# Moving x and the result in one transfer per quarter, and the norm's sums ahead of x times norm_g on GpSimd

## The chip, the core and the metric

The kernel runs on 1 core of one Trainium2 chip. The metric is the device time of one execution in microseconds. The engines go by the names of the profile: PE is TensorE's matmul side and PEld its weight loads, DVE is VectorE, ACT is ScalarE, POOL is GpSimd, and SP issues most of the DMA transfers. An engine's own queue of DMA issues is written SPq, ACTq or POOLq.

## The reference

Four pre-norm residual layers over x of 256 rows and 1024 columns, and one norm at the end. The layers' mixers are pooling, gated DeltaNet, latent attention and pooling again.

```python
def rmsnorm(x, g):
    xf = x.astype(jnp.float32)
    y = xf * lax.rsqrt(jnp.mean(xf * xf, axis=-1, keepdims=True) + EPS)
    return (y * g.astype(jnp.float32)).astype(x.dtype)

for i in range(DEPTH):
    h = rmsnorm(x, norm_g[i])
    y = mixer(i % 3)(h, ...)
    x = x + y.astype(x.dtype)
return rmsnorm(x, final_g)
```

The change touches how x comes in, how the result goes out, and the norm between a layer and the next.

## The kernel before

**Tiles.** x lives in two tiles of 128 partitions, `xs[0]` and `xs[1]` (named x_93 and x_94 in the listings of instructions below), 1024 columns and one more. Partitions 0 to 63 hold the even rows of a block of 128, partitions 64 to 127 the odd ones. Half a tile, 512 columns, is called a quarter of x here, written x(t,c) for tile t and column half c. Every number that is multiplied on TensorE is split into a high and a low part: ACT makes `whi` (or `hTh`) by a cast, DVE the difference `wlo` (or `hTl`), and three matmuls replace one.

**Order of the work.** The program is written for all engines in one order, with `later(...)` putting a piece of it behind a given instruction. A scheduler then sorts each engine's instructions by a simulated time. So an edit in one place may also change the order elsewhere. Each engine works its own list strictly in order.

**Start.** `load_x` (line 304) issues two transfers per quarter on SP's queue, each of 64 rows. Between the quarters stand the first weight units (`prefetch`, line 1348): the first projection, the gate of pooling group 3, takes its 8 row blocks of weights as units 0 to 3 of one block each (256 KB) and units 4 and 5 of two (512 KB). `First.feed` (line 355) transposes a quarter on TensorE (line 359) and splits it (lines 242 and 247). The square sums of the four quarters (line 256) run on ACT between weight splits (line 153).

**End of a layer.** `layer_out` (line 445) makes the output projection in two column halves. For the second half the result comes in two pieces of 256 columns per tile. As soon as a piece is complete, DVE adds it to x (line 450), and `part_done` (line 285) adds its squares: ACT squares and sums (line 256), POOL works on the sum of one number per partition. With the first piece of a tile's second half POOL also computes `half`: a multiplication by D (line 297) and a root (line 298), stored in the extra column of x, so that the last square sum, over 257 columns, comes out complete. `Normed.begin` (line 382) multiplies x by norm_g on POOL for 256 columns, called `hg`, and `Normed.rest` (line 388) takes the inverse root `xr` on POOL (line 390) and multiplies by it: two pieces on ACT (line 402) and two on DVE (line 397).

**The result.** `Final.feed` (line 437) is the same norm with final_g. For each of the two tiles it issues four transfers on SP's queue (line 442): two column halves of 64 even and 64 odd rows.

Of the kernel before, what the change touches and what calls it, by code (L numbers as in the profile page):

```python
# [13 lines left out]
ALU = mybir.AluOpType  # L14
# [3 lines left out]
D = 1024  # L18
S = 256
NT = S // P  # L20
KD = D // P
CW = 512
CUT = 256
KU = 2
EPS = 1e-6
# [17 lines left out]
def trunk(ctx: ExitStack, tc: tile.TileContext, x, positions, norm_g, pool_w_in, pool_w_grp,  # L43
          pool_scale, pool_w_out, gdn_w_in, gdn_conv, gdn_a_log, gdn_dt_bias, gdn_norm_g,
          gdn_w_out, mla_w_in, mla_q_norm_g, mla_w_uq, mla_kv_norm_g, mla_w_ukv, mla_w_out,
          final_g, out, depth=4, final=True):
    nc = tc.nc
# [28 lines left out]
    def small(name, *dims, bufs=2):  # L76
        return sm.tile([P, *dims], F32, tag=name, name=name, bufs=bufs)
# [4 lines left out]
    def later(*instructions):  # L82

        order = ExitStack()
        for ins in instructions:
            order.enter_context(tc.issue_after(ins))
        return order


    mark = {}  # L90
# [74 lines left out]
    def unpaired(o, ps, n=CW):  # L165

        return halves(o, n), parted(ps, n)
# [86 lines left out]
    def sumsq(src, n, o, scale=1.0):  # L254
        junk = wh.tile([P, CW + 1], F32, tag="junk", name="junk", bufs=1)
        nc.scalar.activation(junk[:, :n], src, AF.Square, scale=scale, accum_out=o)
# [25 lines left out]
    xs = [const.tile([P, D + 1], F32, name=f"x{t}") for t in range(NT)]  # L282
    ms = [None] * NT

    def part_done(t, a, n, apart=False):
        s = small(f"ms{t}{a // 256}", 1)
        end = a + n == D
        more = int(end and not apart)
        with later(*[m for e, m in mark.items() if e == "rest"]):
            sumsq(xs[t][:, a:a + n + more], n + more, s, scale=float(D) ** -0.5)  # L290
        if a == 0:
            nc.gpsimd.tensor_scalar(s, s, EPS, None, ALU.add)
        elif not more:
            nc.gpsimd.tensor_tensor(out=s, in0=s, in1=ms[t], op=ALU.add)
        ms[t] = s
        if a and not end:
            nc.gpsimd.tensor_scalar(s, s, float(D), None, ALU.mult)
            nc.gpsimd.tensor_tensor(out=xs[t][:, D:], in0=s, in1=half, op=ALU.pow)

    def by_row(a, t):  # L300

        return a[0, t * P:(t + 1) * P, :].rearrange("(a b) c -> b a c", b=2)

    def load_x(t, c):
        sl = slice(c * CW, (c + 1) * CW)
        for b in range(2):
            nc.sync.dma_start(out=xs[t][b * 64:(b + 1) * 64, sl], in_=by_row(x, t)[b, :, sl])

    load_x(0, 0)
    grow = small("grow", P, bufs=1)[:KD]  # L310
    nc.scalar.dma_start(out=grow, in_=norm_g[0].rearrange("(k p) -> k p", p=P))
# [4 lines left out]
    half = const.tile([P, 1], F32, name="half")  # L316
# [23 lines left out]
    class First:  # L340
# [14 lines left out]
        def feed(self, t, c):  # L355
            ps = bank(tps, "tp")
            for b in range(4):
                a = c * CW + b * P
                nc.tensor.transpose(ps[:, b * P:(b + 1) * P], xs[t][:, a:a + P], ident)
            return split_out((ps.rearrange("p (b s) -> p b s", b=4),  # L360
                              self.hT.many(4 * c, 4, t * P, P), None))
# [63 lines left out]
    def cols_of(w, c0, cols=CW):  # L425
        v = w.rearrange("(k p) c -> p k c", p=P)
        return lambda k0, n: v[:, k0:k0 + n, c0:c0 + cols]
# [5 lines left out]
    class Final(Normed):  # L433
# [3 lines left out]
        def feed(self, t):  # L437
            y = self.rest(t) if final else [xs[t][:, :CW], xs[t][:, CW:D]]
            for c in range(2):
                sl = slice(c * CW, (c + 1) * CW)  # L440
                for b in range(2):
                    nc.sync.dma_start(out=by_row(out, t)[b, :, sl],
                                      in_=y[c][b * 64:(b + 1) * 64])

    def layer_out(w, yT, ks, i, gain=None):

        def done(t, a, ps):
            n = ps.shape[1]
            xv, pv = unpaired(xs[t][:, a:a + n], ps, n)
            nc.vector.tensor_tensor(out=xv, in0=pv, in1=xv, op=ALU.add)  # L450
            part_done(t, a, n)

        project(cols_of(w, 0), ks, yT, done=lambda t, c, ps: done(t, 0, ps), gain=gain)
        with later(mark["sp"]):
            nxt = LayerIn(i + 1) if i + 1 < depth else Final()
        for t in range(NT):
            nxt.begin(t, 0)

        def last(t, c, ps):
            done(t, CW + c * CUT, ps)  # L460
            if c == 0:
                nxt.begin(t, CW)
            else:
                nxt.feed(t)

        project(cols_of(w, CW), ks, yT, tail=3, cuts=CW // CUT, done=last, gain=gain)
        return nxt
# [885 lines left out]
    nxt = First()  # L1353
    nxt.columns()
    turn = nxt.feed(0, 0)
    with later(*turn):
        prefetch(0)
        warming(WARM[1])
        prefetch(1)
    load_x(1, 0)  # L1360
    with later(mark["act"], mark["dve"]):
        turn = nxt.feed(1, 0)
    with later(*turn):
        prefetch(2)
        prefetch(3)
        part_done(0, 0, CW, apart=True)
    load_x(0, 1)
    load_x(1, 1)
    with later(mark["act"], mark["dve"]):
        turn = nxt.feed(0, 1)  # L1370
        turn += nxt.feed(1, 1)
    with later(*turn):
        prefetch(4)
        part_done(1, 0, CW, apart=True)
        part_done(0, CW, CW, apart=True)
        prefetch(5)
        part_done(1, CW, CW, apart=True)
    for i in range(depth):
        nxt = layers[i % 3](i, i // 3, nxt.hT)
# [31 lines left out]
```

## Time and profile before

| | us |
|---|---|
| median of 3 runs (lowest to highest) | 828.32 (827.48 to 829.5) |
| the profiled execution's own time | 832.1 |
| its span, first to last instruction | 830.4 |
| PE busy | 799.4 (96%) |
| DVE busy | 603.4 (73%) |
| ACT busy | 492.9 (59%) |
| POOL busy | 159.8 (19%) |
| DMA, mean over the span | 168 GB/s |

A line of a timeline gives the start, the length, the engine, the line of the kernel, the operation, output and input tiles, their shape, a count, and in brackets how long the engine had been idle and for what. A line of a tile or line view gives the shortest, median and longest duration in ns, and when the first and the last started. A DMA issue is given with the size and the median time from issue to landing. PE's matmuls overlap, so its busy share says less than which wait ends last. The granted clock of the profiled execution was 0.986 of full speed.

### The profile page before, as it was taken

The numbers are of one execution on the slowest core, as the hardware profiler recorded it, in microseconds if no ns is written. First come the engines' busy times: TensorE is split into PE (matmuls) and PEld (weight loads), VectorE is DVE, ScalarE is ACT, GpSimd is POOL, SyncE is SP. The second block draws the span as 40 slices with busy tenths as digits, with TensorE's granted clock in tenths as the row PEclk, the third lists the DMA queues.
The fourth block names the chain that finished last, engine by engine and source line by source line (L and its number), as shares of the span: only waits on it lengthen the run. The fifth ranks groups of instructions, "written<-read, shape, count | busy, mean of one in ns | idle before, by whom it ended". The sixth has DMA issues, their size and how long they took to land.

```text
span 830.4 us, 16162 instructions
## 1 busy us (share of the span) xinstructions
PE 799.4 (96%) x5966; PEld 758.0 (91%) x5966; DVE 603.4 (73%) x1141; ACT 492.9 (59%) x993; POOL 159.8 (19%) x296
## 2 busy tenths in 40 slices
PE   8989999999898979999999999999999999999996
PEld 7989988989898978788989999999999989999996
DVE  4699887666987967356666678778877767877772
ACT  6665565567855655255566564666665565566662
POOL 2001100334236992023121112000000120000012
PEclk9999999999999989899999999999999999999998
DMA  6865666756655544303647786653552547576662
GB/s 204 224 180 167 193 209 210 221 153 195 193 135 180 163 139 118 124 12 115 187 125 224 231 180 185 192 164 102 153 175 80 179 143 214 183 223 202 202 204 51
DMA packets 109079, 139.90 MB, mean 168 GB/s; under 512 B 21316, under 2 KB 51208, under 8 KB 109000
## 3 DMA queue, kind: packets, MB, share of 16 engines
q1 hardware_dynamic: 106608, 137.12, 55.0%
q0 software_dynamic: 528, 1.58, 0.6%
q8 instruction: 47, 0.77, 0.4%
q10 hardware_dynamic: 1864, 0.17, 0.2%
q14 instruction: 32, 0.26, 0.1%
HBM read 137.27 MB, written 1.58 MB: 167 GB/s over the span
## 4 chain that ended last, share of the span: by engine, by line
PE 67%; DVE 11%; POOL 8%; DMA 8%; issue 4%; ACT 2%; SPq 0%; POOLq 0%; DVEq 0%; ACTq 0%
PE acc L162 53%; PE aux L162 7%; POOL pr L846 3%; DVE wlo L154 3%; POOL Tb L850 2%; DMA raw<-in_pool_w_out_dram 2%; DVE wlo L150 1%; DMA raw<-in_pool_w_in_dram 1%; DVE win L551 1%; DMA T<-d_t 1%; DMA Lb<-d_l 1%; DVE h L397 1%; DMA Gb<-d_g 1%; PE aux L979 1%; PE tp L1314 1%
## 5 line engine op out<-in xcount | busy, mean ns | idle before, releaser
L150 DVE TENSOR_TENSOR wlo<-raw,whi 128x512 fp32r<-128x512 f32 (+1 forms) x366 | 254.2, 719 | 104.3 <-ACT whi L149 100.8
L149 ACT CAST whi<-raw 128x512 fp32r<-128x512 f32 (+1 forms) x380 | 223.7, 617 | 167.6 <-PE acc L162 82.3
L162 PE MATMUL acc<-hTh,whi 128*128 128x256 f32 x832 | 230.7, 278 | 2.3 <-ACT gsg L670 1.5
L162 PE MATMUL acc<-hTl,whi 128*128 128x256 f32 x832 | 231.2, 278 | 0.0
L162 PE MATMUL acc<-hTh,wlo 128*128 128x256 f32 x832 | 229.8, 277 | 0.0
L162 PEld LDWEIGHTS acc<-hTh,whi 128*128 128x128 f32 x832 | 160.7, 193 | 2.9 <-ACT gsg L670 1.7
L162 PEld LDWEIGHTS acc<-hTl,whi 128*128 128x128 f32 x832 | 160.8, 193 | 0.3
L162 PEld LDWEIGHTS acc<-hTh,wlo 128*128 128x128 f32 x832 | 160.7, 193 | 0.1
L162 PE MATMUL acc<-wlo,yTh 128*128 128x256 f32 (+1 forms) x384 | 112.7, 312 | 0.8 <-DVE wlo L154 0.8
L162 PE MATMUL acc<-whi,yTh 128*128 128x256 f32 (+1 forms) x384 | 112.3, 315 | 0.0
L162 PE MATMUL acc<-whi,yTl 128*128 128x256 f32 (+1 forms) x384 | 89.1, 313 | 0.0
L162 PEld LDWEIGHTS acc<-wlo,yTh 128*128 128x128 f32 x384 | 73.2, 191 | 4.8 <-DVE wlo L154 1.7
L162 PEld LDWEIGHTS acc<-whi,yTh 128*128 128x128 f32 x384 | 72.9, 191 | 3.1
L162 PEld LDWEIGHTS acc<-whi,yTl 128*128 128x128 f32 x384 | 63.1, 191 | 3.4
L154 DVE SCALAR_TENSOR_TENSOR wlo<-raw,colsT,whi 128x512 fp32r<-128x512 f32 x64 | 47.0, 769 | 21.1 <-ACT whi L153 20.7
L153 ACT ACTIVATE whi<-raw,gain 128x512 fp32r<-128x512 f32 x64 | 43.6, 720 | 31.1 <-DMA raw<-in_pool_w_in_dram 22.6
L153 ACT ACTIVATE whi<-raw,colsT 128x512 fp32r<-128x512 f32 x64 | 43.5, 720 | 30.9 <-DMA raw<-in_pool_w_out_dram 18.0
L385 POOL TENSOR_TENSOR hg<-x,gain 128x256 f32<-128x256 f32 x16 | 13.4, 850 | 244.1 <-DVE x L450 244.1
L162 PE MATMUL acc<-wlo,hTh 128*128 128x512 f32 (+1 forms) x144 | 54.8, 385 | 1.9 <-DVE wlo L150 1.3
L154 DVE SCALAR_TENSOR_TENSOR wlo<-raw,gain,whi 128x512 fp32r<-128x512 f32 x64 | 46.6, 748 | 11.1 <-ACT whi L153 11.1
L162 PE MATMUL acc<-whi,hTh 128*128 128x512 f32 (+1 forms) x144 | 52.7, 379 | 0.7 <-ACT hTh L242 0.7
L162 PE MATMUL acc<-whi,hTl 128*128 128x512 f32 (+1 forms) x144 | 42.5, 373 | 0.0
(364 smaller groups left out, 1530.9 us busy)
## 6 DMA issues: line engine op xcount, KB each, us to landing
raw<-in_pool_w_in_dram SPq DMA_DIRECT2D x62, 512.0 KB, 4.4
raw<-in_gdn_w_in_dram SPq DMA_DIRECT2D x48, 512.0 KB, 4.0
raw<-in_pool_w_out_dram SPq DMA_DIRECT2D x32, 512.0 KB, 4.4
raw<-in_mla_w_in_dram SPq DMA_DIRECT2D x24, 512.0 KB, 4.5
raw<-in_mla_w_uq_dram SPq DMA_DIRECT2D x36, 256.0 KB, 3.4
raw<-in_pool_w_grp_dram SPq DMA_DIRECT2D x16, 512.0 KB, 3.8
raw<-in_gdn_w_out_dram SPq DMA_DIRECT2D x16, 512.0 KB, 3.8
raw<-in_mla_w_ukv_dram SPq DMA_DIRECT2D x32, 256.0 KB, 3.3
```

Source lines behind the costliest of these rows:

```text
L149: a = nc.scalar.copy(hi, v)
L150: b = e.tensor_tensor(out=lo, in0=v, in1=hi.bitcast(F32), op=ALU.subtract)
L153: a = nc.scalar.activation(hi, v, AF.Copy, scale=g)
L154: b = e.scalar_tensor_tensor(out=lo, in0=v, scalar=g, in1=hi.bitcast(F32), op0=ALU.mult, op1=ALU.subtract)
L162: return nc.tensor.matmul(inorder(o, n), lhsT=lhs, rhs=woven(rhs, n), start=start, stop=stop)
L385: nc.gpsimd.tensor_tensor(out=self.early[t, a], in0=xs[t][:, sl], in1=self.g[:, sl], op=ALU.mult)
L397: nc.vector.scalar_tensor_tensor(out=h[:, cut:], in0=xs[t][:, sl], scalar=r[:, 0:1], in1=self.g[:, sl], op0=ALU.mult, op1=ALU.mult)
L551: nc.vector.tensor_tensor(out=nxt[:, :, d:], in0=cur[:, :, d:], in1=cur[:, :, :S - d], op=ALU.add)
L846: nc.gpsimd.tensor_tensor(out=pv, op=ALU.mult, in0=Lb[:, r, r + 1:, None].to_broadcast([M * Q, n, c]), in1=Tb[:, r:r + 1, :c].to_broadcast ...
L850: mark["blocks"] = nc.gpsimd.tensor_tensor(out=tv, in0=tv, in1=pv, op=ALU.subtract).ins
L979: nc.tensor.matmul(ps[:, c], lhsT=U[0][:, h, :], rhs=vR[h // 2][:, 0, c * DV:(c + 1) * DV], start=True, stop=True)
L1314: nc.tensor.transpose(ps[:, a * P:(a + 1) * P], sb[:, a * P:(a + 1) * P], ident)
```

## The change

Each quarter of x now comes in by one transfer of 128 rows, and each quarter of the result goes out by one. The last quarter of the result is issued on ACT's queue, all others on SP's. Of the square sums, all but those that end a row (or belong to the first layer) are left unscaled, with EPS times D added to the first, so that the multiplication by D falls away. And the second `hg` of a tile is placed behind the instruction that stores the root.

```diff
@@ part_done
         end = a + n == D
         more = int(end and not apart)
+        unit = 1.0 / D if end or apart else 1.0
         with later(*[m for e, m in mark.items() if e == "rest"]):
-            sumsq(xs[t][:, a:a + n + more], n + more, s, scale=float(D) ** -0.5)
+            sumsq(xs[t][:, a:a + n + more], n + more, s, scale=unit ** 0.5)
         if a == 0:
-            nc.gpsimd.tensor_scalar(s, s, EPS, None, ALU.add)
+            nc.gpsimd.tensor_scalar(s, s, EPS * D * unit, None, ALU.add)
         elif not more:
             nc.gpsimd.tensor_tensor(out=s, in0=s, in1=ms[t], op=ALU.add)
         ms[t] = s
         if a and not end:
-            nc.gpsimd.tensor_scalar(s, s, float(D), None, ALU.mult)
-            nc.gpsimd.tensor_tensor(out=xs[t][:, D:], in0=s, in1=half, op=ALU.pow)
+            mark["sofar"] = nc.gpsimd.tensor_tensor(out=xs[t][:, D:], in0=s, in1=half,
+                                                    op=ALU.pow).ins
@@ load_x
-        for b in range(2):
-            nc.sync.dma_start(out=xs[t][b * 64:(b + 1) * 64, sl], in_=by_row(x, t)[b, :, sl])
+        nc.sync.dma_start(out=xs[t][:, sl], in_=by_row(x, t)[:, :, sl])
@@ Final.feed
-                for b in range(2):
-                    nc.sync.dma_start(out=by_row(out, t)[b, :, sl],
-                                      in_=y[c][b * 64:(b + 1) * 64])
+                queue = nc.scalar if c and t == NT - 1 else nc.sync
+                queue.dma_start(out=by_row(out, t)[:, :, sl], in_=y[c])
@@ layer_out, last
             if c == 0:
-                nxt.begin(t, CW)
+                with later(mark.pop("sofar")):
+                    nxt.begin(t, CW)
```

`by_row` (line 300) views 128 rows of a DRAM tensor as 2 (even, odd) by 64 by columns. Before, the index b took one of the two, so that 64 by 512 was left; now the whole pattern of 2 by 64 by 512 stands against 128 by 512 on the SBUF side.

At the start of the program on SP's queue stood, before the change (x_93 and x_94 are the two tiles of x, raw a weight unit):

```order
L307 DMA x_93<-in_x_dram 64x512 x2
L133 DMA raw<-in_pool_w_in_dram 128x512
L307 DMA x_94<-in_x_dram 64x512 x2
L133 DMA raw<-in_pool_w_in_dram 128x512 x2
L307 DMA x_93<-in_x_dram 64x512 x2
L133 DMA raw<-in_pool_w_in_dram 128x512
L307 DMA x_94<-in_x_dram 64x512 x2
L133 DMA raw<-in_pool_w_in_dram 128x2x512 x14
```

And with the change, at the same place of SP's queue:

```order
L307 DMA x_93<-in_x_dram 128x1x512
L133 DMA raw<-in_pool_w_in_dram 128x512
L307 DMA x_94<-in_x_dram 128x1x512
L133 DMA raw<-in_pool_w_in_dram 128x512
L307 DMA x_93<-in_x_dram 128x1x512
L133 DMA raw<-in_pool_w_in_dram 128x512 x2
L307 DMA x_94<-in_x_dram 128x1x512
L133 DMA raw<-in_pool_w_in_dram 128x2x512 x14
```

There are four issues fewer, and the third quarter now stands ahead of the third weight unit instead of behind it.

On POOL, at the end of the DeltaNet layer, stood before the change (hg is x times the gain, ms the square sum, the x row the root that is stored beside x, xr the inverse root):

```order
L385 TENSOR_TENSOR hg<-x_93,gain 128x256
L294 TENSOR_TENSOR ms_5250<-ms_5250,ms_5005 128x1
L297 TENSOR_SCALAR ms_5250<-ms_5250 128x1
L298 TENSOR_TENSOR x_93<-ms_5250,half 128x1
L390 TENSOR_TENSOR xr<-ms_5277,neghalf 128x1
L385 TENSOR_TENSOR hg<-x_94,gain 128x256
L294 TENSOR_TENSOR ms_5325<-ms_5325,ms_5016 128x1
L297 TENSOR_SCALAR ms_5325<-ms_5325 128x1
L298 TENSOR_TENSOR x_94<-ms_5325,half 128x1
L390 TENSOR_TENSOR xr<-ms_5352,neghalf 128x1
```

With the change, at the same place of POOL's list:

```order
L295 TENSOR_TENSOR ms_5244<-ms_5244,ms_4999 128x1
L298 TENSOR_TENSOR x_93<-ms_5244,half 128x1
L385 TENSOR_TENSOR hg<-x_93,gain 128x256
L390 TENSOR_TENSOR xr<-ms_5270,neghalf 128x1
L295 TENSOR_TENSOR ms_5318<-ms_5318,ms_5010 128x1
L298 TENSOR_TENSOR x_94<-ms_5318,half 128x1
L385 TENSOR_TENSOR hg<-x_94,gain 128x256
L390 TENSOR_TENSOR xr<-ms_5344,neghalf 128x1
```

The multiplication is gone, and hg has moved from ahead of the sum to behind the root, directly ahead of xr. The three other layer ends read the same.

## The prediction

> **What bounds the kernel now.** I read the page first (span, chain of waits), then the DMA queues and issues, then the timeline of the first 22 us and the last 15 us, then busy time by stretches for the stretches that the change touches.
>
> ```profile
> span 830.4 us, 16162 instructions
> PE 67%; DVE 11%; POOL 8%; DMA 8%; issue 4%; ACT 2%; SPq 0%; POOLq 0%; DVEq 0%; ACTq 0%
> 21.00:162.00 141.00, 137.34 (x1101) 132.21 (x1100) 117.00 (x192) 86.27 (x134) 13.59 (x17) 1.00 0.66 200
> ```
>
> TensorE carries the chain, so what the change can move lies where TensorE waits for something: at the start for x, at three layer ends for the norm, and after TensorE's last matmul for the norm and the stores. The row of a stretch gives its length, then busy time of PE, PEld, DVE, ACT and POOL, the clock, the DMA share and GB/s. Behind 21 us the first layer has little slack: of 141 us PE is busy 137.3, so that some 3.7 us of a late start can be won back there, if its gaps all close.
>
> **The transfers: on how many DMA engines do they run?** Before, a quarter of x (128 rows of 512 numbers) is two transfers of 64 rows each. After, it is one, whose DRAM side counts 2 (even and odd rows), then 64, then 512, and whose SBUF side counts 128, then 512. Whether all 16 DMA engines still share it is the question on which the rest hangs, and ScalarE's small transfers say something on it:
>
> ```profile
> q10 hardware_dynamic: 1864, 0.17, 0.2%
> crow<-in_gdn_conv_dram ACTq DMA_DIRECT2D x1, 64.0 KB, 4.3
> bw<-in_gdn_w_in_dram ACTq DMA_DIRECT2D x1, 64.0 KB
> rows<-in_pool_scale_dram ACTq DMA_DIRECT2D x2, 8.0 KB, 4.0
> posi<-in_positions_dram ACTq DMA_DIRECT2D x2, 0.5 KB, 2.8
> grow<-in_norm_g_dram ACTq DMA_DIRECT2D x1, 4.0 KB
> rows<-in_mla_q_norm_g_dram ACTq DMA_DIRECT2D x1, 3.0 KB
> rows<-in_mla_kv_norm_g_dram ACTq DMA_DIRECT2D x1, 2.0 KB
> rows<-in_gdn_norm_g_dram ACTq DMA_DIRECT2D x1, 1.0 KB
> alog<-in_gdn_a_log_dram ACTq DMA_DIRECT2D x1, 4.0 KB
> dtb<-in_gdn_dt_bias_dram ACTq DMA_DIRECT2D x1, 4.0 KB, 4.2
> ```
>
> These are all the transfers of queue q10. One packet per contiguous piece makes 128 (crow) + 1024 (bw) + 2×16 + 2×128 (posi, single numbers) + 8 + 6 + 4 + 2 + 128 + 128 = 1716. The queue has 1864, so 148 remain. Were there one closing packet per engine used and always 16 engines, 12 transfers would make 192. With as many engines as there are rows, up to 16, they make 148: 96 for crow, bw, alog, dtb and the two posi, 32 for the two of pool_scale, and 8 + 6 + 4 + 2. That is exactly what is there. So a transfer of 2 rows ran on 2 engines. No transfer of this kernel has unlike outer counts on its two sides, so that 2 against 128 also gives 2 is an inference: the DRAM side has only two outer pieces to deal out. I take 2 engines.
>
> The Trainium skill, "DMA: Bandwidth & Descriptors", section "Why a DMA increments its semaphore by 16 and not by 1", says the same in general: the slowest dimension longer than one of each side is looked at, and the largest number up to 16 that divides both is used. The 148 packets agree for equal sides; no run shows unlike ones so far. Against it stands the same page's rule for kernel authors (section "Rules for kernel authors") that two transfers to the two halves of the partitions serialize anyway and should be one of 128: by that rule alone the sum would be the first rival's.
>
> What one engine moves, and the start and the end of the program:
>
> ```profile
> 12.00:14.00 2.00, 2.00 (x11) 1.73 (x11) 1.35 (x2) 0.76 (x2) 0.00 (x0) 1.00 1.03 372
> 822.00:824.50 2.50, 0.56 (x5) 0.36 (x4) 0.42 (x1) 0.61 (x4) 1.71 (x5) 1.00 0.96 206
> 0.80 1.23 SPq L307 DMA_DIRECT2D x<-in_x_dram  x2
> L307 SPq DMA_DIRECT2D x<-in_x_dram x8: 466/584/597, 0.8 to 7.3; - x8
> DMA to landing us min/median/max: 2.7/4.3/5.5
> 4.32 1.09 PE L359 MATMUL tp<-ident,x 128*128 128x128 f32 x4 [0.50 <-DMA x<-in_x_dram]
> 13.81 0.60 PE L359 MATMUL tp<-ident,x 128*128 128x128 f32 x4
> 14.45 0.59 ACT L242 CAST hTh<-tp 128x512 fp32r<-128x512 f32 x1 [1.69 <-PE tp L359]
> 14.93 1.34 ACT L153 ACTIVATE whi<-raw,gain 128x512 fp32r<-128x512 f32 x2
> 16.17 0.62 ACT L256 ACTIVATE junk<-x 128x512 f32<-128x512 f32 x1
> 16.69 0.20 ACT L256 ACTIVATION_READ_ACCUMULATOR junk<-x 128x1 f32 x1
> 16.78 1.33 ACT L153 ACTIVATE whi<-raw,gain 128x512 fp32r<-128x512 f32 x2
> 20.23 0.75 DVE L154 SCALAR_TENSOR_TENSOR wlo<-raw,gain,whi 128x512 fp32r<-128x512 f32 x1
> 21.59 0.27 PE L162 MATMUL acc<-hTh,whi 128*128 128x256 f32 x1
> ```
>
> From 12 to 14 us, with whole-height weight loads, all 16 engines are busy (share 1.03) and move 372 GB/s: 23.3 GB/s each, 88 ns for a row of 2 KB. In the first four stores it is 206/(16×0.96) = 13.4 GB/s, 153 ns a row. A quarter on two engines is 64 rows each: 5.6 us by the first, 9.8 by the second; a 256 KB weight unit is 8 rows on each of 16, 0.70 us. I take 88 ns for both directions: each of two engines has a half of the partitions to itself, while in the old stores 16 engines crowd on one half at a time. 153 ns is kept for the range.
>
> **Start.** The fastest half quarter lands 2.7 us after its issue; without its 4 rows per engine that is 2.35 us of fixed time. On SP's queue now stand x(0,0), unit 0, x(1,0), unit 1, x(0,1), units 2 and 3, x(1,1), units 4 and 5; units behind a quarter need the same two engines for their share and wait for it. x(0,0), issued at 0.80, lands at 0.80 + 2.35 + 5.63 = 8.8 (before, TensorE began on it at 4.3). x(1,1) lands 3 quarters and 4 units later: 8.8 + 16.9 + 2.8 = 28.5; units 4 and 5 at 29.9 and 31.3 (1.41 each). Behind x(1,1) stand, in ScalarE's order, the cast (0.59), two splits (1.34), a square sum (0.82), two splits (1.33), then the last difference on VectorE (0.75): with the transposes' 0.60 that is 33.9, and 0.6 for the last matmuls gives 34.5 for the end of the first projection. Before, the first matmul behind it started at 21.59. **+12.9 us.** Bounds: 9.2, if the 3.7 us of slack above all help; 15.2, if from the cast on everything takes as long as before (14.45 to 21.59, 7.1 us, from 29.7). The four issues that SP saves (0.58 each) lie in that wait and bring nothing.
>
> **Norm at the layer ends.** The last rows of the program show the pattern, which is the same code at each layer end; the row of hg over the whole program is with them:
>
> ```profile
> 821.59 0.42 ACT L256 ACTIVATE junk<-x 128x256 f32<-128x256 f32 x1 [0.40 <-DVE x L450]
> 821.92 0.19 ACT L256 ACTIVATION_READ_ACCUMULATOR junk<-x 128x1 f32 x1
> 821.64 0.73 POOL L385 TENSOR_TENSOR hg<-x,gain 128x256 f32<-128x256 f32 x1 [1.39 <-DVE x L450]
> 822.34 0.19 POOL L294 TENSOR_TENSOR ms<-ms,ms 128x1 f32<-128x1 f32 x1
> 822.62 0.23 POOL L297 TENSOR_SCALAR ms<-ms 128x1 f32<-128x1 f32 x1
> 822.93 0.56 POOL L298 TENSOR_TENSOR x<-ms,half 128x1 f32<-128x1 f32 x1
> 822.59 0.42 DVE L450 TENSOR_TENSOR x<-acc,x 128x256 f32<-128x256 f32 x1 [1.09 <-PE acc L162]
> L385 POOL TENSOR_TENSOR hg<-x,gain x16: 733/738/1201, 149.3 to 821.6; 128x256 f32<-128x256 f32 x16
> 824.11 0.55 POOL L390 TENSOR_TENSOR xr<-ms,neghalf 128x1 f32<-128x1 f32 x1 [0.62 <-ACT junk L256]
> ```
>
> Now the sum needn't wait for hg: it starts at 822.2 (square sum read at 822.11), the root 0.28 later and ends at 823.05, hg follows to 823.8. The last square sum may start with x at 823.05 instead of 823.52 and ends by 823.7; but xr, on the same engine, now waits for hg, so it starts at 823.85 instead of 824.11: **0.26 us** won, not the 0.5 that the multiply and the place of hg suggest. hg is the next late thing, and behind it on GpSimd stands xr, for which ScalarE's and VectorE's h wait. If hg takes the 1.2 us that its slowest took, 0.2 is lost instead. Three layer ends give −0.8 (from −1.5 to +0.6). At the fourth it is worth nothing, since the stores of the first rows still hold the two engines. The scheduler has also put some VectorE and ScalarE rows of the first two layers in another order; I take 0 for it, with bounds of 3 us to either side, four 128x512 differences of 0.75.
>
> **End.**
>
> ```profile
> 824.69 1.00 ACT L402 ACTIVATE h<-hg,xr 128x256 f32<-128x256 f32 x2 [0.66 <-POOL xr L390]
> 820.85 6.79 SPq L442 DMA_DIRECT2D out_dram<-h  x8
> out_dram<-h SPq DMA_DIRECT2D x8, 128.0 KB, 2.3
> ```
>
> Before, the last of eight issues starts 0.6 us before 827.6 and lands 2.3 us later: 829.3. After, two stores go out at 820.85 and two (one by ScalarE's queue) at about 825.3 and 825.8, as the two halves of h end, when the first two still run. Fixed time is 2.3 less 4 rows of 153 ns, 1.7; then four quarters one behind the other on the same two engines: 820.85 + 1.7 + 22.5 = 845.1. **+15.8 us**; at 153 ns 820.85 + 1.7 + 39.2 = 861.8, +32.5. A second queue doesn't help, since the engines and not the issuing are late.
>
> **Sum.** 830.4 + 12.9 − 0.8 + 15.8 = 858.3. The profiled execution took 832.1, 3.8 more than the median of 828.3; the same 27.9 on the median gives **856.2 us**. Own range of this case: 852 (start 9.2) to 875 (start 15.2, stores at 153 ns).
>
> **Rivals.**
>
> 1. *The transfers are spread over 16 engines after all*, as when the SBUF side's 128 rows decide. Nothing in the trace rules it out. The second x quarter is then issued two issues earlier, 1.2 us, and TensorE starts that much earlier; at the end the last issue starts when ScalarE's h is done, at 825.75 instead of 827.0; four layer ends give 1.0: 828.3 − 3.4 = 824.9, faster. Chance 0.12. The point from which it decides: 8 engines or more, where a quarter takes 1.4 us or less, no longer than two issues.
> 2. *One direction only*, if the destination's or the source's shape alone decides. Stores on two engines alone: 828.3 + 15.8 − 1.2 − 0.8 = 842.1; loads alone: 828.3 + 12.9 − 1.2 − 1.0 = 839.0. 0.08.
> 3. *Each transfer gets another pair of engines.* Then the four overlap. x(1,1), issued at about 4.4, lands at 12.4, hardly later than before (7.3 + 5.5 = 12.8); x(0,0) and x(1,0) are 2 to 4 us late in a stretch where they aren't last, say +1.5; the last store, 825.8 + 1.7 + 5.6 = 833.1, is +3.8: with −0.8, 832.8. Nothing speaks for it but that the engine numbers aren't in the trace. 0.06. The skill's same section gives such a transfer the lowest-numbered engines, which speaks against it; no run here shows the numbers.
>
> **How the numbers follow.** Two engines in both directions 0.74. Slower by over 0.3% (about what a measurement can tell from no change; 825.8 to 830.8): the main case, rivals 2 and 3, 0.88. Rival 1 alone can be faster: 0.09, and 0.03 of it falls within 0.3%. The range reaches from rival 2's 838 to 875 and leaves out rivals 1 and 3, 0.18.
>
> **What would show it.** In the changed profile: x landing 8 us after issue in the median instead of 4.3 and growing to over 20; TensorE idle on x until about 28; few DMA engines busy (share near 0.13) with 47 GB/s in the last 20 us; out_dram landing 7 us and more. Wrong would be: landings under 4 us, a store phase that ends within 5 us of TensorE's last matmul, or hg still ahead of the sum on GpSimd.

## The result, and the profile after

| | median of the runs, us | lowest to highest |
|---|---|---|
| before | 828.91 | 827.48 to 832.24 |
| changed | 867.32 | 864.02 to 871.11 |

The ratio is 1.046 (95% interval 1.041 to 1.051): slower by 38.4 us, where 27.9 were forecast and the range was 852 to 875. The profiled execution of the changed kernel took 868.0 us, its span is 35.9 us longer than before. From its page:

```profile
span 866.3 us, 16121 instructions
PE 68%; DMA 11%; POOL 7%; DVE 6%; issue 3%; ACT 2%; SPq 1%; ACTq 0%; DVEq 0%; POOLq 0%
q10 hardware_dynamic: 1994, 0.43, 0.2%
```

The chain's DMA share has grown from 8 to 11%. Queue q10 has 130 packets more than before, and the one new transfer on it, the last store, has 128 rows of 2 KB. So two closing packets remain: the store of 128 rows ran on two engines. That was an inference in the prediction; this row shows it.

**Start.** TensorE's transposes of the four quarters of x, and SP's issues (start, length, engine, line, operation, tiles, count, and in brackets the idle time before and what ended it):

```profile
9.12 1.12 PE L359 MATMUL tp<-ident,x 128*128 128x128 f32 x4 [5.29 <-DMA x<-in_x_dram]
15.52 1.12 PE L359 MATMUL tp<-ident,x 128*128 128x128 f32 x4 [4.43 <-DMA x<-in_x_dram]
21.43 1.11 PE L359 MATMUL tp<-ident,x 128*128 128x128 f32 x4 [4.37 <-DMA x<-in_x_dram]
28.44 1.12 PE L359 MATMUL tp<-ident,x 128*128 128x128 f32 x4 [2.00 <-DMA x<-in_x_dram]
...
2.63 3.70 SPq L133 DMA_DIRECT2D raw<-in_pool_w_in_dram  x1
6.38 0.55 SPq L307 DMA_DIRECT2D x<-in_x_dram  x1
6.97 5.60 SPq L133 DMA_DIRECT2D raw<-in_pool_w_in_dram  x2
12.62 0.64 SPq L307 DMA_DIRECT2D x<-in_x_dram  x1
```

The quarters are there every 6 to 7 us, the last at 28.4 (28.5 was forecast). The other rows were not foreseen: an issue of a weight unit, 0.37 us in the median of the program, takes 3.70 us, and two take 5.60 (one of them 5.03), so that x(1,1) is issued only at 12.6.

**End.** The last tile, and the stretch from 843 to 864 us (its length, busy time of PE, PEld, DVE, ACT and POOL, clock, DMA share, GB/s):

```profile
841.91 9.22 SPq L442 DMA_DIRECT2D out_dram<-h  x3
844.79 0.55 POOL L390 TENSOR_TENSOR xr<-ms,neghalf 128x1 f32<-128x1 f32 x1
850.02 0.51 ACT L402 ACTIVATE h<-hg,xr 128x256 f32<-128x256 f32 x1 [5.31 <-DMA out_dram<-h]
855.08 0.51 ACT L402 ACTIVATE h<-hg,xr 128x256 f32<-128x256 f32 x1 [4.55 <-DMA out_dram<-h]
855.75 0.65 ACTq L442 DMA_DIRECT2D out_dram<-h  x1
...
843.00:864.00 21.00, 0.62 (x6) 0.43 (x4) 1.39 (x3) 1.70 (x6) 1.98 (x4) 0.61 0.13 48
```

A DMA share of 0.13 and 48 GB/s are two engines of 16, busy throughout (0.13 and 47 were forecast). New is who waits: the last tile's h needs the buffers of the first tile's h, and these come free only when the first stores have landed.

**In between.** The second xr of each layer end marks the end of a layer. Before:

```profile
170.16 0.55 POOL L390 TENSOR_TENSOR xr<-ms,neghalf 128x1 f32<-128x1 f32 x1 [0.62 <-ACT junk L256]
424.30 0.55 POOL L390 TENSOR_TENSOR xr<-ms,neghalf 128x1 f32<-128x1 f32 x1 [0.62 <-ACT junk L256]
671.81 0.55 POOL L390 TENSOR_TENSOR xr<-ms,neghalf 128x1 f32<-128x1 f32 x1 [0.62 <-ACT junk L256]
```

Changed:

```profile
184.33 0.55 POOL L390 TENSOR_TENSOR xr<-ms,neghalf 128x1 f32<-128x1 f32 x1
442.97 0.55 POOL L390 TENSOR_TENSOR xr<-ms,neghalf 128x1 f32<-128x1 f32 x1 [0.24 <-ACT junk L256]
692.88 0.55 POOL L390 TENSOR_TENSOR xr<-ms,neghalf 128x1 f32<-128x1 f32 x1
```

With the fourth at 824.11 before and 844.79 now, the changed kernel is late by 14.2, 18.7, 21.1 and 20.7 us at the four layer ends, and by 35.9 at the end of the span. The first and the last step, 14.2 and 15.2, are the ones that the prediction summed (12.9 − 0.3 and 15.8). The second layer's 4.5 and the third layer's 2.4 it did not have. In the second layer, DeltaNet, TensorE now has a wait that wasn't there, for the result T of the triangular solve (called the solve from here on), which GpSimd works out from a tile Lb and sends to T by DMA:

```profile
328.11 3.65 PE L938 MATMUL aux<-T,LT 128*128 128x64 f32 x16 [11.35 <-DMA T<-d_t]
```

### The profile page after: what moved, and what is told of

Same layout as the page of the kernel before. It is cut to its first block, busy times and chain, and to the rows that moved or that the text cites. A ratio compares the mean times of both kernels' runs of the same rounds, so it can differ in the third digit from the quotient of the medians.

```text
span 866.3 us, 16121 instructions
## 1 busy us (share of the span) xinstructions
PE 802.9 (93%) x5966; PEld 759.8 (88%) x5966; DVE 600.4 (69%) x1141; ACT 493.9 (57%) x993; POOL 160.2 (18%) x288
## 4 chain that ended last, share of the span: by engine, by line
PE 68%; DMA 11%; POOL 7%; DVE 6%; issue 3%; ACT 2%; SPq 1%; ACTq 0%; DVEq 0%; POOLq 0%
PE acc L162 54%; PE aux L162 7%; POOL Tb L850 3%; POOL pr L846 2%; DMA raw<-in_pool_w_out_dram 2%; DMA x<-in_x_dram 2%; DMA raw<-in_gdn_w_in_dram 2%; DMA out_dram<-h 1%; DVE wlo L150 1%; DVE wlo L154 1%; SPq L133 1%; DMA raw<-in_pool_w_in_dram 1%; DMA Lb<-d_l 1%; DMA Gb<-d_g 1%; PE aux L938 1%
## 5 line engine op out<-in xcount | busy, mean ns | idle before, releaser
L150 DVE TENSOR_TENSOR wlo<-raw,whi 128x512 fp32r<-128x512 f32 (+1 forms) x366 | 250.4, 711 | 94.6 <-ACT whi L149 91.4
L153 ACT ACTIVATE whi<-raw,colsT 128x512 fp32r<-128x512 f32 x64 | 44.2, 720 | 31.2 <-DMA raw<-in_pool_w_out_dram 20.7
L154 DVE SCALAR_TENSOR_TENSOR wlo<-raw,gain,whi 128x512 fp32r<-128x512 f32 x64 | 46.7, 748 | 19.4 <-ACT whi L153 17.1
L385 POOL TENSOR_TENSOR hg<-x,gain 128x256 f32<-128x256 f32 x16 | 13.6, 862 | 208.5 <-DVE x L449 208.5
```

What stands on the lines that cost most here:

```text
L150: b = e.tensor_tensor(out=lo, in0=v, in1=hi.bitcast(F32), op=ALU.subtract)
L153: a = nc.scalar.activation(hi, v, AF.Copy, scale=g)
L154: b = e.scalar_tensor_tensor(out=lo, in0=v, scalar=g, in1=hi.bitcast(F32), op0=ALU.mult, op1=ALU.subtract)
L385: nc.gpsimd.tensor_tensor(out=self.early[t, a], in0=xs[t][:, sl], in1=self.g[:, sl], op=ALU.mult)
```

## The experiments

My theory after the result: the DRAM side's count of 2 sets the number of engines and with it start and end; the rest comes from another program order. Its rivals: the transfer is slow for another reason (its walk over DRAM, or that it covers all partitions); the loss in the layers follows from the late start. In the tables, each kernel stands beside the runs of the kernel before on the same chip.

### Each part alone

`loads_only` is the kernel before with this edit alone:

```diff
-        for b in range(2):
-            nc.sync.dma_start(out=xs[t][b * 64:(b + 1) * 64, sl], in_=by_row(x, t)[b, :, sl])
+        nc.sync.dma_start(out=xs[t][:, sl], in_=by_row(x, t)[:, :, sl])
```

> The kernel before with only the loads of x merged. Two engines: x(1,1) lands at 28 us again, the first projection ends 13 to 16 us late; with the program order's 5 us to either side, 842 us (837 to 848). If the queue's order rather than the engines' number held the changed kernel's start, the same. If only the stores were slow, 829.

`stores_only` has only the edit of `Final.feed`:

```diff
-                for b in range(2):
-                    nc.sync.dma_start(out=by_row(out, t)[b, :, sl],
-                                      in_=y[c][b * 64:(b + 1) * 64])
+                queue = nc.scalar if c and t == NT - 1 else nc.sync
+                queue.dma_start(out=by_row(out, t)[:, :, sl], in_=y[c])
```

> The kernel before with only the stores merged and the last one on ScalarE's queue. Two engines: the stores take 23 us from the first issue on and not 8, so 844 us (839 to 849 with the program order's 5 us). Whether a second queue gives a second pair of engines shows in the landings: 5 us apart means the same pair, landings in pairs means another pair and 834 us.

`norm_only` has only the edits of `part_done` and `last`, as the diff of the change shows them.

> The kernel before with only the norm's part of the change. The root now starts ahead of hg, xr 0.3 to 0.8 us sooner at each of three layer ends: 826.5 to 828 us if nothing else moves; the scheduler writes the later layers in another order, which may be worth 5 us to either side. If the reordering in the changed kernel comes from this part, the second layer's wait on the triangular solve (11 us there) shows here too and the time is 833.

| kernel | us | before | ratio (95%) |
|---|---|---|---|
| loads_only | 842.19 | 829.56 | 1.015 (1.012 to 1.019) |
| stores_only | 844.64 | 829.56 | 1.018 (1.016 to 1.020) |
| norm_only | 833.96 | 829.56 | 1.006 (1.004 to 1.009) |

SP's queue has the packets of the loads, before:

```profile
q1 hardware_dynamic: 106608, 137.12, 55.0%
```

and in `loads_only`:

```profile
q1 hardware_dynamic: 106488, 137.12, 52.8%
```

Eight transfers with 16 closing packets each make 128, four with two make 8: exactly the 120 that are missing. The loads too ran on two engines. They cost 12.6 us and the stores 15.1, each within 1 us of what was expected; rival 2 of the prediction, one direction only, is out. The stores of `stores_only` wait for one another like the changed kernel's: ScalarE's h waits 4.99 and 4.54 us for landings, so the second queue gave no second pair of engines. The surprise is the norm: meant to save 0.8 us, it costs 4.4. The three sum to 32.1 of the 38.4 us; with intervals of 2 to 5 us on these numbers, little of what is missing is sure.

### How many engines

Four kernels keep the changed kernel and alter only the view of DRAM. The rows of x then stand in another order than the computation wants, so that their outputs are not the reference's and only their times mean something. In `deal4`, `deal8` and `deal16` every engine's instructions stand in the very order of the changed kernel:

```diff
-        return a[0, t * P:(t + 1) * P, :].rearrange("(a b) c -> b a c", b=2)
+        return a[0, t * P:(t + 1) * P, :].rearrange("(a b) c -> b a c", b=4)
```

and the same with 8 and 16. `plain_rows` takes the 128 rows as they lie in DRAM; its order differs from the changed kernel's in the first projection, where x(1,1) is issued one weight unit earlier, and behind the first layer it is the same:

```diff
-        return a[0, t * P:(t + 1) * P, :].rearrange("(a b) c -> b a c", b=2)
+        return a[0, t * P:(t + 1) * P, None, :].rearrange("p o c -> o p c")
...
-        nc.sync.dma_start(out=xs[t][:, sl], in_=by_row(x, t)[:, :, sl])
+        nc.sync.dma_start(out=xs[t][:, sl], in_=by_row(x, t)[0, :, sl])
...
-                queue.dma_start(out=by_row(out, t)[:, :, sl], in_=y[c])
+                queue.dma_start(out=by_row(out, t)[0, :, sl], in_=y[c])
```

> The changed kernel with x and the result moved in plain row order, so that the DRAM side of each quarter counts 128 rows and not 2 (the rows of x then stand in another order than the computation wants, and the output is not the reference's). Nearly the same program order as the changed kernel's, above all behind the first layer. If the DRAM side's count of 2 sets the number of DMA engines: x lands in 3 to 5 us, the stores in 2 to 3 us, and both long waits go: the lead at the first layer's end is back to within 2 us of the kernel before, and the stores end within 5 us of TensorE's last matmul. If instead a transfer over all 128 partitions is slow by itself, x still lands at 9 to 28 us and the time stays near 867. For the 7 us that the changed kernel loses in its second and third layers: if the program order causes them, they are still there, 832 us; if they only follow from the late start, they go too, 825 us.

> The changed kernel, instruction for instruction in the same order, but the DRAM side of x and of the result counts 4, then 32 rows, not 2, then 64 (row 4a+b instead of 2a+b goes with partition 32b+a; the rows then stand in another order than the computation wants, and the output is not the reference's). Four engines: a quarter is 32 rows of 84 to 88 ns on each, 2.8 us and not 5.6. x(1,1) lands at 17 us (28.4 on two engines, 10.0 in plain row order), so the first layer ends 6 to 8 us later than in plain row order; the stores take 13 us from the first issue on (23.4 on two, 7.7 in plain order), 5.3 more than there: 843 us (840 to 847). If instead the strided walk over DRAM or a transfer over both halves of the partitions is slow, not the count, the time stays near 867.

> The same with 16, then 8 rows on the DRAM side (output again in another row order). Sixteen engines: as in plain row order, 831 us (828 to 834), with 16 closing packets for the store on ScalarE's queue. If the stride over DRAM costs anything by itself, it is slower than plain row order; if only the walk over both halves mattered, 867.

> The changed kernel in the same program order with 8, then 16 rows on the DRAM side (output again in another row order). Eight engines, 16 rows of 84 ns on each: 1.35 us for a quarter. My prediction put the point from which the change stops costing at 8 engines, where a quarter takes no longer than two issues: then this is as fast as sixteen engines, 833 us (830 to 836). If instead each row on an engine costs the same along the whole curve, from 867.3 on two engines (64 rows) to 832.8 on sixteen (8 rows), 0.62 us a row, it is 838 us (836 to 841).

The row of queue q10 for 4, 8 and 16:

```profile
q10 hardware_dynamic: 1996, 0.43, 0.3%
```

```profile
q10 hardware_dynamic: 2000, 0.43, 0.3%
```

```profile
q10 hardware_dynamic: 2008, 0.43, 0.3%
```

| rows on DRAM's outer side | closing packets | us | before | ratio (95%) | x(0,0) on TensorE at | last xr to the end |
|---|---|---|---|---|---|---|
| 2 (changed) | 2 | 867.32 | 828.91 | 1.046 (1.041 to 1.051) | 9.12 | 21.5 |
| 4 | 4 | 852.09 | 829.48 | 1.027 (1.023 to 1.031) | 6.48 | 14.5 |
| 8 | 8 | 840.09 | 829.96 | 1.013 (1.010 to 1.016) | 5.63 | 8.8 |
| 16 | 16 | 832.80 | 829.48 | 1.006 (1.002 to 1.009) | 4.17 | 5.7 |
| 128 (plain_rows) | 16 | 830.97 | 829.56 | 1.002 (1.000 to 1.004) | 3.75 | 4.8 |

The packets less 1864 and less the store's 128 are 2, 4, 8 and 16: the number of engines is the smaller outer count, up to 16. All these counts divide 128, so the runs don't tell the smaller count from a common divisor. The walk over DRAM costs little, if anything: the intervals for 16 and 128 overlap, and the 3.2 us by which the first 256-wide matmul comes later with 16 (22.3 us against 19.1 in the profiles) can be the other order of issues. A transfer over both halves of the partitions is as quick as two, given 16 engines. This is what the Trainium skill, "DMA: Bandwidth & Descriptors", section "Why a DMA increments its semaphore by 16 and not by 1", says (the largest number up to 16 that divides the slowest dimension of both sides); with these runs it is shown for unlike sides. The advice of the same page of the Trainium skill, in "Rules for kernel authors", to make one transfer of two to the two halves of the partitions, cost 12.6 us at the loads and 15.1 at the stores here, where the DRAM side counts 2; in `plain_rows`, where it counts 128, merging costs nothing that shows.

`deal8` was the test of the threshold that the prediction gave, 8 engines. It falls: 840 us, near the straight line of 0.62 us per row on an engine (838), not 833. Some 3 of the 7 us that it is above `deal16` are at its end; the rest the two profiles don't show, whose first layers end at 170.5 and 170.8 us. And `deal4` is 9 us above its expectation of 843. Some 4 of them are in its second layer (256.6 us against 252.9 in plain row order, though the order is the same there): half of TensorE's busy time at half clock, which the next part takes up, is 8.7 us there and 4.8 in plain row order. The others are at the end, where the buffers show:

```profile
834.74 0.55 POOL L390 TENSOR_TENSOR xr<-ms,neghalf 128x1 f32<-128x1 f32 x1
838.10 0.51 ACT L402 ACTIVATE h<-hg,xr 128x256 f32<-128x256 f32 x1 [3.45 <-DMA out_dram<-h]
840.61 0.51 ACT L402 ACTIVATE h<-hg,xr 128x256 f32<-128x256 f32 x1 [1.99 <-DMA out_dram<-h]
841.28 0.66 ACTq L442 DMA_DIRECT2D out_dram<-h  x1
```

I had let the four stores follow one another on busy engines, 13 us from the first issue. But the second tile's h waits for the first tile's landings, its stores start late, and the first issue at 831.86 lies 17.3 us before the end at 849.2. On two engines the same wait is covered, since the engines still have 5 us of queue. In `deal8` it is 1.42 and 0.79 us, in `deal16` none: the cost ends only where a landing takes no longer than the next tile's norm.

### Where the layers lose

`norm_math` has of the norm's edits only the folding of the multiplication by D, `norm_place` only the place of x times norm_g:

```diff
 norm_math
+        unit = 1.0 / D if end or apart else 1.0
...
-            sumsq(xs[t][:, a:a + n + more], n + more, s, scale=float(D) ** -0.5)
+            sumsq(xs[t][:, a:a + n + more], n + more, s, scale=unit ** 0.5)
...
-            nc.gpsimd.tensor_scalar(s, s, EPS, None, ALU.add)
+            nc.gpsimd.tensor_scalar(s, s, EPS * D * unit, None, ALU.add)
...
-            nc.gpsimd.tensor_scalar(s, s, float(D), None, ALU.mult)
 norm_place
-            nc.gpsimd.tensor_tensor(out=xs[t][:, D:], in0=s, in1=half, op=ALU.pow)
+            mark["sofar"] = nc.gpsimd.tensor_tensor(out=xs[t][:, D:], in0=s, in1=half,
+                                                    op=ALU.pow).ins
...
-                nxt.begin(t, CW)
+                with later(mark.pop("sofar")):
+                    nxt.begin(t, CW)
```

> The kernel before with only the multiplication by D folded away; x times norm_g keeps its place ahead of the sum. In the program order TensorE's four transposes of kqT ahead of the triangular solve's result stand where the norm's whole change has them, earlier by some ten rows than before. If the loss of the norm's change is that order, it is here too: 832 to 834 us, with TensorE waiting 10 us or more on the solve's result, the solve near 48 us, the third layer near 249.8 us. If the loss comes from x times norm_g standing later, this is 828 us.

> The kernel before with only the place of x times norm_g changed, behind the root; the multiplication by D stays. The transposes of kqT stand as before. If the order around the solve is the loss, this has none: 827 to 829 us, the solve near 45 us, the third layer near 247.5 us. If the place of x times norm_g is the loss, 833.

`with_mult` is the changed kernel with the multiplication put back:

```diff
-            sumsq(xs[t][:, a:a + n + more], n + more, s, scale=unit ** 0.5)
+            sumsq(xs[t][:, a:a + n + more], n + more, s, scale=float(D) ** -0.5)
...
-            nc.gpsimd.tensor_scalar(s, s, EPS * D * unit, None, ALU.add)
+            nc.gpsimd.tensor_scalar(s, s, EPS, None, ALU.add)
...
         if a and not end:
+            nc.gpsimd.tensor_scalar(s, s, float(D), None, ALU.mult)
```

> The changed kernel with only the multiplication by D put back; the transfers stay on two engines and x times norm_g stays behind the root. In the program order the transposes of kqT stand as before the change. If the program order that comes with the folded multiplication explains what my sum lacked, the time falls by the 7.7 us that folding it alone cost the kernel before (837.2 against 829.5): 859.6 us (856 to 863), with the solve near 45 us, the third layer near 247.5 us, and the start and the end as late as in the changed kernel. If the loss in the second and third layers follows from the late start, it stays at 867.

| kernel | us | before | ratio (95%) | solve | layer 2 | layer 3 |
|---|---|---|---|---|---|---|
| norm_math | 837.24 | 829.48 | 1.010 (1.007 to 1.014) | 48.3 | 256.5 | 250.8 |
| norm_place | 827.06 | 829.48 | 0.998 (0.996 to 1.000) | 45.3 | 251.4 | 247.1 |
| with_mult | 855.99 | 828.88 | 1.033 (1.029 to 1.036) | 44.5 | 253.1 | 247.1 |
| changed | 867.32 | 828.91 | 1.046 (1.041 to 1.051) | 47.9 | 258.6 | 249.9 |

(Solve: first product of Lb to last row of Tb on GpSimd; layers: from second xr to second xr; all from one profile each.) Folding a multiplication of 0.23 us costs 7.8 us (3 us above the 832 to 834 that were expected), and taking the fold out of the changed kernel gives 11.3 back, although its start and end stay as late (first 256-wide matmul at 34.8 us, end 21.3 us behind the last xr). The order did it, not the late start; that rival is out. The loss is in two places, the second layer and the third.

For the second layer the trace shows why. In every profile with the multiplication (before, loads_only, stores_only, norm_place, with_mult, place_two_queues) the view of the tile Lb, the solve's input, names ScalarE among those who wait for it; in every one without (the eight others) it does not. (kqT holds a half of the layer's keys or queries; it and Lb take their buffers from one pool, so that a kqT may have to wait until GpSimd is done with Lb.) Before:

```profile
who waited for it (us, times):
  POOL pr L846: 14.5, 1
  ACT kqT L787: 5.5, 1
```

ScalarE's kqT has there to wait for the end of the solve, and TensorE's transposes of kqT with it (4.67 us in the row below); without the multiplication the scheduler's order lets them go ahead. TensorE's wait, then busy time of PE, PEld, DVE, ACT and POOL during the solve and in the stretch behind it, in which T arrives, in `norm_place`:

```profile
296.85 0.69 PE L795 MATMUL tp<-ident,kqT 128*128 128x128 f32 x2 [4.67 <-ACT kqT L789]
251.40:296.70 45.30, 37.30 (x326) 36.26 (x324) 39.87 (x77) 27.98 (x60) 40.52 (x63) 0.97 0.51 158
296.70:312.00 15.30, 15.15 (x102) 14.72 (x103) 9.77 (x19) 9.01 (x19) 13.88 (x19) 0.85 0.49 138
```

and in `norm_math`:

```profile
254.10:302.40 48.30, 47.52 (x409) 46.32 (x407) 45.62 (x92) 33.66 (x71) 43.55 (x64) 1.00 0.50 153
302.40:322.00 19.60, 8.24 (x28) 7.30 (x29) 7.74 (x14) 2.66 (x6) 13.07 (x18) 0.56 0.45 134
```

TensorE does 409 matmuls during the solve and not 326, VectorE 45.6 us of work and not 39.9; so far that looks like a gain. But the solve itself becomes 3.0 us longer, and then the cover is used up: TensorE stands still until T is there. The matmuls behind the wait, `norm_math` and `norm_place`:

```profile
313.76 3.65 PE L938 MATMUL aux<-T,LT 128*128 128x64 f32 x16 [12.02 <-DMA T<-d_t]
```

```profile
309.48 1.89 PE L940 MATMUL aux<-T,LT 128*128 128x64 f32 x16
```

The same 16 matmuls take 3.65 us and not 1.89: the wait has cost the clock. In the trace's clock record TensorE is at half clock for 17.1 us around this wait in `norm_math`, 8.2 of them busy; in `norm_place`, around its shorter wait at the solve's end, for 6.8, 4.4 of them busy. So the 12 us are not the price. Over the whole second layer TensorE is idle for 17.2 us in `norm_math` and for 14.2 in `norm_place`, and busy for 239.3 and 237.2: 3.0 us of waiting and 2.1 of longer matmuls make the 5.1 us between them. All half-clock stretches of all profiles are multiples of 3.41 us up to the last matmul, which agrees with the Trainium skill, "TensorE: Matmul & The Clock Gate", Part 1, where an idle window of some 3.4 us halves the clock. Such a stretch comes again behind the next waits, so layer 2 differs by up to 6 us between profiles of the same order (252.9 in plain_rows, 258.6 in the changed kernel): half of the busy time at half clock is 4.8 us in the one and 8.5 in the other, 3.7 of the 5.7 us.

The third layer's loss, 2.2 to 3.7 us, also goes with the folding alone (249.8 to 250.8 in all profiles without the multiplication, 247.1 to 247.6 in all with it). There it is the weights that come late: in all eight profiles without the multiplication the chain of waits has 3.5 to 5.9 us for a weight unit of the next layer near the layer's end, in four of them also about 4 for one of mla_w_out, and in the six with it neither. SP's issues of the last eight units of mla_w_out in `norm_place` and `norm_math`, and the chain's wait in `norm_math`:

```profile
615.40 32.46 SPq L133 DMA_DIRECT2D raw<-in_mla_w_out_dram  x8
623.00 39.35 SPq L133 DMA_DIRECT2D raw<-in_mla_w_out_dram  x8
...
666.39 4.54 DMA raw<-in_pool_w_in_dram
```

The first five issues keep the same distances in both; the last three come 3.7 to 6.9 us later, and most of SP's waiting there (32.0 us against 27.4) is for VectorE's splits of earlier units, which free the buffers of the weights. No run changes the place of these splits by itself.

### x on ScalarE's queue, and what is left

`x_on_act` is the changed kernel with this edit in `load_x`:

```diff
-        nc.sync.dma_start(out=xs[t][:, sl], in_=by_row(x, t)[:, :, sl])
+        nc.scalar.dma_start(out=xs[t][:, sl], in_=by_row(x, t)[:, :, sl])
```

> The changed kernel with the four loads of x issued on ScalarE's queue, so that no weight stands behind them in SP's queue; still two engines. If x alone sets the start, x(1,1) lands at 28 us or, sharing its engines with the weights, up to 31, and the time is 867 (864 to 870). If the weights queued behind x are what comes last, they are there at 10 us now, and the first layer ends up to 4 us sooner: 863. ScalarE then should be held at its own issues (3.7 and 5.6 us in SP's queue before).

It took 869.78 us, the kernel before 828.88: ratio 1.049 (1.046 to 1.053), no better than the changed kernel. ScalarE's issues, and TensorE's last quarter:

```profile
3.04 4.97 ACTq L307 DMA_DIRECT2D x<-in_x_dram  x1
8.04 5.89 ACTq L307 DMA_DIRECT2D x<-in_x_dram  x1
...
31.90 0.66 PE L359 MATMUL tp<-ident,x 128*128 128x128 f32 x4 [0.67 <-DMA x<-in_x_dram]
```

The last quarter is there 3.5 us later than behind SP's weights. From there to the first 256-wide matmul it takes 7.6 us, against 8.4 in the changed kernel and 6.8 in `with_mult`, although SP had issued its first weight units from 0.8 us on. So the weights behind x were not what came last, x was. And the long issues follow the two-engine transfers to the other queue: there the third and fourth transfer of x are held, on SP's queue it was the weight issues behind them.

`place_two_queues` is `norm_place` with the last tile's second half stored by ScalarE's queue, still in halves of 64 rows:

```diff
                 for b in range(2):
-                    nc.sync.dma_start(out=by_row(out, t)[b, :, sl],
-                                      in_=y[c][b * 64:(b + 1) * 64])
+                    queue = nc.scalar if c and t == NT - 1 else nc.sync
+                    queue.dma_start(out=by_row(out, t)[b, :, sl],
+                                    in_=y[c][b * 64:(b + 1) * 64])
```

> What the experiments leave of the change: the transfers by halves of 64 rows on 16 engines, the multiplication by D where it was, x times norm_g behind the root, and the last tile's second half stored by ScalarE's queue. From 827.1 the second queue takes two of the last four issues, 0.57 us each, off SP: the end is 5.2 us behind the last xr instead of 6.3: 826 us (824 to 828). If the landing and not the issuing is last there, 827.

It took 827.49 us against 828.88: 0.999 (0.997 to 1.000). The end is 6.1 us behind the last xr, not 5.2: the second queue gives nothing. `norm_place` alone, 827.06 against 829.48, has an interval that reaches 1.000, so no version here is shown to beat the kernel before.

## Why the prediction was right or wrong

**Two engines: right**, in both directions, by the closing packets and by the dose of 2, 4, 8, 16. A row of 2 KB takes 84 ns in the stores' packets, so 88 ns was the right choice and 153 ns, the range's upper end, did not occur. Rivals 1 to 3 are out, with one remark: in plain row order the change is rival 1 come true, and it is 831 and not 825. The cost of the folded multiplication's order would explain the difference, but no run has plain row order without it.

**Start: right mechanism, some 2 us too small.** x(1,1) came at 28.4 (28.5). The first 256-wide matmul followed at 34.8 in `with_mult` (34.5 forecast) and at 36.9 in the changed kernel, whose order differs. What failed is the 3.7 us of slack that was named as the lower bound's reason: at most 1.1 of it came back. At that matmul the changed kernel, `with_mult` and `loads_only` are 15.3, 13.2 and 13.6 us late, at the first layer's end 14.2, 14.4 and 15.8. The step "units behind a quarter need the same two engines for their share and wait for it" was right in its times but is not what decides (`x_on_act`); that SP would be held at its issues was missing, and cost nothing that shows, since x(1,1) came when it was forecast.

**Norm: wrong.** The shift of x times norm_g did what was worked out, and a little more: from xr to xr at a layer end 4.41 to 4.46 us in `with_mult` and 4.85 to 4.89 before at the first three ends, 0.43 won at each where 0.26 was forecast. The failing step is "I take 0 for it, with bounds of 3 us to either side", for the reordering. The bounds came from a few moved differences of 0.75 us; but what the order decides is whether a wait is covered, here TensorE's on T, with the half clock behind it, and in the third layer the wait for weight units. The term measures 7.8 us alone and 11.3 on top of the rest.

**End: right**, 21.5 us instead of 6.3 behind the last xr, +15.2 against +15.8. The two stores of the second tile were not issued at 825.3 and 825.8 plus the delay, as put there, but only after the first tile's landings freed the buffers of h. On two engines the queue hides that, so the sum came out right for a reason that was not quite mine. That a second queue would not help was right.

**The sum** of 27.9 us is what the change costs without the folded multiplication: `with_mult` is 27.1 us above the kernel before. The folded multiplication is the rest. That it costs more there than alone is not shown: with the intervals of the ratios it is 11 us, give or take 5, against 8, give or take 3. That the result still lies inside the range is luck: its upper end stood for stores at 153 ns a row, which did not happen, and not for the 3 us that were allowed for the order.

## What to carry to other kernels

Before two transfers are merged into one, look at the outermost count of both sides: the smaller one decided here how many engines moved it, and the packets of the queue tell (data pieces plus one closing packet for each engine). Where a scheduler orders the program, an edit as small as one dropped multiplication has to be followed to the longest waits that are just covered, and a reordering's bound is the size of those waits (for a result or for a weight unit) and the half clock after them, not the size of the instructions that moved. Putting one such edit back into the changed kernel tells it from the rest in a single run.

## What the runs showed of the hardware that was not expected

- An issue can be held. With two-engine transfers in the queue a weight issue took 3.70 us and two took 5.60 on SP's queue, and single issues of x 4.97 and 5.89 us on ScalarE's, where 0.4 to 0.7 is usual. On four engines none of SP's first nine issues took over 0.8 us, but the tenth took 3.41 (`deal4`); on eight and on sixteen none of the first twelve took over 1 us. Why an issue is held no run shows.
- The solve's GpSimd instructions of a given shape last differently: the first 64x112 subtraction took 0.42 us before and 1.59 in the changed kernel, while other instructions of the solve took up to 1.6 in both. The whole solve took 44.5 to 45.3 us where VectorE had 39.9 to 41.2 us of work beside it (before, norm_place, with_mult) and 47.8 to 48.3 where it had 45.6 to 47.0 (changed, norm_math, norm_only, plain_rows). That VectorE's work is the cause is only argued.
